# First mixer of a two-layer trunk: silu in one instruction for eight convolution tiles, the softplus chain behind them, q's products of both token tiles ahead of rotary and turns

## The chip, the cores and the metric

The kernel runs on one core of a Trainium2 chip. The metric is the device time of one execution in microseconds. The kernel before takes 1034.35 us, the median of three runs (1034.08 to 1034.95).

## The reference

A decoder trunk of two layers works on 256 tokens of width 1024, in float32. Each layer is half a SwiGLU block, a mixer, and another half block, all added to the residual. The change lies in the first mixer alone:

```
z, xbc, dt, q_a, kv_a = split(h @ w_in)
xbc = silu(causal_conv4(xbc) + conv_b)          # 2048 channels: xs 1024, B 512, C 512
dt  = softplus(dt + dt_bias)                    # 16 heads
y   = ssd(xs, dt, -exp(a_log), B, C) + d_skip * xs
y   = rms_norm_by_group(y * silu(z))
q   = rope(rms_norm(rms_norm(q_a) @ w_q_b))     # 8 heads of 96, the last 32 rotary
k,v = rms_norm(kv_c) @ w_kv_b ...               # 8 heads of 64 + 32 shared rotary, 8 of 64
o   = causal_softmax_attention(q, k, v)
out = concat(y, o) @ w_out
```

In ssd, the decay between two tokens of a chunk of 128 is exp(acs[i] − acs[j]), where acs is the running sum of dt·A within the chunk.

## The kernel before

Activations lie as 128 tokens by channels (two token tiles, t = 0 and 1) or turned as 128 channels by 256 tokens. A float32 product is made of three products of two-part operands (high and low part, names ending in h and l, or wh and wl for weights); ScalarE casts the high part of each weight tile (L77) and VectorE makes the low part (L80).

In the first mixer the work goes in this order. The products into q_a and kv_a (two token tiles). Then convolution tiles: `xbc(c)` makes one of 16 channel tiles, 24 matmuls of 256 columns into a bank p_xbc; `conv_silu` (L441) reads it: ScalarE writes cv (Identity with scale and bias, L446), VectorE adds three taps (L448), ScalarE takes Tanh (L451), VectorE makes (tanh + 1)·v (L452). The convolution's weights are halved beforehand, so v is half of the convolution and (tanh v + 1)·v is silu of the whole. Tiles 8 to 11 are B (tile BT), 12 to 15 are C (tile CT), 0 to 7 are xs (tile xT).

Between them stand the products of q by heads (bank p_qb, two per token tile, L279 to L281, each read by Square L532, the copy qnat L534 and the copy qr L535), the rotary step on POOL, the turns m_qT, the products of k and v (p_kvb) and their turns m_kT.

The softplus chain: Abs (L395) and Exp (L398) on ScalarE, a polynomial of nine VectorE steps (L402), dts, a (L587), the matmul m_acs (L590) that sums a over the chunk, the turn m_acsT, ScalarE's copy acsT (L597), and a transfer on POOL's queue to acs_rows in DRAM (L599). From there two transfers per token tile (L657, POOL's queue) spread the rows of 8 heads each to all partitions as E. On E ScalarE does 16 Relus of one head each (L663) and four Exps (L666), VectorE multiplies by the products CB (L669), and TensorE uses it in m_yd (L703).

Attention goes by token tile: scores m_sc into PSUM banks of 512 columns (two buffers; 4 heads a bank for t = 0, 2 heads for t = 1), the maximum on VectorE, Exp on ScalarE (p, L629), 1/den on VectorE and the product by it on POOL (L424), turns m_pT, then m_att_o.

Later the z products (p_z, four tiles of 512 columns), their gates (ScalarE Tanh L715, VectorE L716), the gated norm, and the product out of the mixer (p_acc, L323 to L325), which reuses the banks of z.

All instructions of one engine run in order. The order is not the program's: a scheduler that simulates a timeline puts each engine's instructions in a row and hands out buffers, and `self.order(a, b)` adds that a comes after b. So an edit at one place can move instructions at another.

Of the kernel before, what the change touches and what calls it, by code (L numbers as in the profile page):

```python
# [11 lines left out]
AF = mybir.ActivationFunctionType  # L12
# [3 lines left out]
P = 128  # L16
# [18 lines left out]
ROW = {}  # L35
# [50 lines left out]
class Net:  # L86
# [351 lines left out]
        return pt  # L438


    def conv_silu(self, c, b, out):  # L441

        nc = self.nc
        cw = self.conv[:, c, :]
        v = self.small([P, S], "cv", bufs=3)
        nc.scalar.activation(out=v, in_=b, func=AF.Identity, scale=cw[:, 3:4], bias=cw[:, 4:5])  # L446
        for s in (1, 2, 3):
            nc.vector.scalar_tensor_tensor(out=v[:, s:], in0=b[:, :S - s], scalar=cw[:, 3 - s:4 - s], in1=v[:, s:],  # L448
                                           op0=ALU.mult, op1=ALU.add)
        th = self.small([P, S], "cth", bufs=2)  # L450
        self.tanh = nc.scalar.activation(out=th, in_=v, func=AF.Tanh)  # L451
        return nc.vector.scalar_tensor_tensor(out=out, in0=th, scalar=1.0, in1=v, op0=ALU.add, op1=ALU.mult)  # L452
# [12 lines left out]
    def mixer0(self, hT, x, after):  # L465
        nc, st, row = self.nc, self.st, self.row
# [5 lines left out]
        dtv = self.small([P, 2, 16], "dtv")  # L472
# [5 lines left out]
        for t in range(2):  # L478
            c = slice(t * P, (t + 1) * P)
# [8 lines left out]
            squares = nc.scalar.activation(out=junk[:, :32], in_=pk[:, 256:], func=AF.Square, accum_out=ssn[:, t, 2:3])  # L488
            nc.vector.tensor_scalar(out=ssn[:, t, 0:2], in0=ssn[:, t, 0:2], scalar1=EPS, scalar2=None, op0=ALU.add)
            self.power(rsn[:, t, :], ssn[:, t, 0:2])  # L490
            qn = self.blk([P, 640], "qn", grp="a")
# [12 lines left out]
        BC = [self.blk([P, 4, S], n) for n in ("BT", "CT")]  # L504

        def xbc(c, out):
            w = st.load([D])[0]
            b = self.bank([P, S], "xbc")
            self.in_ch(b, hT, w)
            return self.conv_silu(c, b, out)  # L510
        for i in range(4):
            xbc(8 + i, BC[0][:, i, :])

# [4 lines left out]
        qT = [self.blk([96, 8, P], f"qT{t}", grp="a") for t in range(2)]  # L518
        kT = [self.blk([96, 8, P], f"kT{t}", grp="a") for t in range(2)]
        sq = self.small([P, 2, 8], "sqs")  # L520
        for t in range(2):
            qn = self.blk([P, 8, 96], "qnat", grp="a")
            qr = self.blk([P, 8, 2, 16], "qr")
            for j in range(2):
                b = self.bank([P, 4, 96], "qb")
                bf = b.rearrange("p a b -> p (a b)")
                for k in range(3):
                    self.mm_tok(bf, lambda k: (qaT[0][:, k, :], qaT[1][:, k, :]), [k], t,
                                [(wq[k][0][:, j * 384:(j + 1) * 384], wq[k][1][:, j * 384:(j + 1) * 384])], k == 0, k == 2)
                hs = slice(4 * j, 4 * j + 4)  # L530
                junk = self.small([P, 512], "junk")[:, :384].rearrange("p (a b) -> p a b", a=4)
                nc.scalar.activation(out=junk, in_=b, func=AF.Square)  # L532
                nc.vector.tensor_reduce(out=sq[:, t, hs], in_=junk, op=ALU.add, axis=X)
                nc.scalar.copy(out=qn[:, hs, :64], in_=b[:, :, :64])  # L534
                nc.scalar.copy(out=qr[:, hs, :, :], in_=b[:, :, 64:].rearrange("p a (s d) -> p a s d", s=2))  # L535
            roped = self.apply_rope(qn[:, :, 64:].rearrange("p a (s d) -> p a s d", s=2), qr, t, "q", 8)

            nc.vector.tensor_scalar(out=sq[:, t, :], in0=sq[:, t, :], scalar1=96 * EPS, scalar2=None, op0=ALU.add)
            self.power(sq[:, t, :], sq[:, t, :])
            self.order(self.pow, roped)  # L540
            for j in range(2):
                tp = self.tbank([96, 4, P], "qT", "a")
                for i in range(4):
                    self.transpose(tp[:, i, :], qn[:, 4 * j + i, :])
                nc.scalar.copy(out=qT[t][:, 4 * j:4 * j + 4, :], in_=tp)
        xbc(12, BC[1][:, 0, :])
        wkv = st.load([D, D])
        for t in range(2):
# [6 lines left out]
            for j in range(2):  # L555
                b = self.bank([P, 4, P], "kvb")
# [16 lines left out]
            for j in range(2):  # L573
# [2 lines left out]
                    self.transpose(tp[:, i, :], kn[:, 4 * j + i, :])  # L576
                nc.scalar.activation(out=kT[t][:, 4 * j:4 * j + 4, :], in_=tp, func=AF.Copy, scale=self.kgain)


        e = self.small([P, 2, 16], "dte")  # L580
        l1 = self.log1p_exp(dtv, e, "dtl", squares)
        dts = self.edge.tile([P, 2, 16], F32, tag="dts", name="dts", bufs=1)
        nc.vector.scalar_tensor_tensor(out=dts, in0=dtv, scalar=0.0, in1=l1, op0=ALU.max, op1=ALU.add)
        ea = self.small([P, 16], "ea")
        nc.scalar.activation(out=ea, in_=row[:, ROW["a_log"]], func=AF.Exp)
        a = self.small([P, 32], "a")
        nc.vector.scalar_tensor_tensor(out=a.rearrange("p (t h) -> p t h", t=2), in0=dts, scalar=-1.0,  # L587
                                       in1=ea.unsqueeze(1).broadcast_to([P, 2, 16]), op0=ALU.mult, op1=ALU.mult)
# [10 lines left out]
        nc.gpsimd.dma_start(out=rows, in_=at_)  # L599
        eacs = self.small([P, 16], "eacs")  # L600
        nc.scalar.activation(out=eacs, in_=acs[:, 16:], func=AF.Exp)

        for i in (2, 3):
            xbc(12 + i, BC[1][:, i, :])


        den = self.small([P, 2, 8], "den")
# [3 lines left out]
        def softmax(t):  # L611
            n = 4 >> t
            kw = P * (t + 1)
            pr = [self.blk([P, 8 // (t + 1), kw], f"p{t}", grp="a") for _ in range(t + 1)]
            for j in range(8 // n):
                b = self.sbank([P, n, kw], "sc", "a")
                for i in range(n):
                    h = n * j + i
                    for kb in range(t + 1):
                        mm(b[:, i, kb * P:(kb + 1) * P], qT[t][:, h, :], kT[kb][:, h, :], start=i == 0 and kb == 0, stop=False,  # L620
                           skip_group_check=True)
                mm(b, self.identb, self.mask[:, 2 * P - kw:].unsqueeze(1).broadcast_to([P, n, kw]), start=False, stop=True, skip_group_check=True)
                hs = slice(n * j, n * j + n)
                nc.vector.tensor_reduce(out=mx[:, t, hs], in_=b, op=ALU.max, axis=X)
                nc.vector.scalar_tensor_tensor(out=mx[:, t, hs], in0=mx[:, t, hs], scalar=-1.0, in1=sq[:, t, hs], op0=ALU.mult, op1=ALU.mult)
                for i in range(n):
                    h = n * j + i
                    m = 8 // (t + 1)
                    self.exp = nc.scalar.activation(out=pr[h // m][:, h % m, :], in_=b[:, i, :], func=AF.Exp, scale=sq[:, t, h:h + 1],  # L629
                                                    bias=mx[:, t, h:h + 1], accum_out=den[:, t, h:h + 1])  # L630
                m = 8 // (t + 1)
                h = n * j
                self.normalize(pr[h // m][:, h % m:h % m + n, :], den[:, t, hs])
            for kb in range(t + 1):
                PT[t, kb] = self.turn_probs(lambda h: pr[h // m][:, h % m, kb * P:(kb + 1) * P], kb, f"pT{t}{kb}")
        oT = [self.blk([P, 2, 4, P], f"oT{t}", F32R, grp="a") for t in range(2)]
        exps = []
        for t in range(2):
            softmax(t)
            exps.append(self.exp)  # L640
            self.attend(t, lambda b, h: PT[t, b][:, h, :], lambda b, h: V[:, b, h, :],
                        (oT[t][:, 0], oT[t][:, 1]))
# [66 lines left out]
        for j in range(2):  # L709
            wz = [s for _ in range(2) for s in st.load([D, D])]  # L710
            for t in range(2):
                b = self.bank([P, 512], "z")
# [39 lines left out]
        for j, (s, hs) in enumerate(cols):  # L752
            nc.gpsimd.tensor_tensor(out=hv(xd[0][:, s]), in0=hv(xd[0][:, s]), in1=dec[:, hs].unsqueeze(2).broadcast_to([P, 8, 64]), op=ALU.mult)
            b = self.sbank([P, 512], "st", "b")
# [3 lines left out]
        for j, (s, hs) in enumerate(cols):  # L758
            b = self.sbank([P, 512], "yo", "b")
# [414 lines left out]
```

## Time and profile before

| | us |
|---|---|
| median of three runs | 1034.35 |
| the profiled execution | 1034.39 |
| its span, first to last instruction | 1032.6 |
| TensorE busy | 1011.2 |
| VectorE busy | 686.0 |
| ScalarE busy | 568.6 |
| POOL busy | 83.8 |

The profile is of one execution. Busy time counts an engine's instructions; what is left of TensorE's span, 21.4 us, is idle time, and the view of waits says on which line it stood and which instruction released it. A timeline lists an engine's instructions by start; a bracket behind a row gives the idle time before it and its releaser. The granted TensorE clock was 0.997 of 2.4 GHz on average.

### The profile page before, as it was taken

The numbers are of one execution on the slowest core, as the hardware profiler recorded it, in microseconds if no ns is written. First come the engines' busy times: TensorE is split into PE (matmuls) and PEld (weight loads), VectorE is DVE, ScalarE is ACT, GpSimd is POOL, SyncE is SP. The second block draws the span as 40 slices with busy tenths as digits, with TensorE's granted clock in tenths as the row PEclk, the third lists the DMA queues.
The fourth block names the chain that finished last, engine by engine and source line by source line (L and its number), as shares of the span: only waits on it lengthen the run. The fifth ranks groups of instructions, "written<-read, shape, count | busy, mean of one in ns | idle before, by whom it ended". The sixth has DMA issues, their size and how long they took to land.

```text
span 1032.6 us, 15136 instructions
## 1 busy us (share of the span) xinstructions
PE 1011.2 (98%) x5609; PEld 866.7 (84%) x5609; DVE 686.0 (66%) x1056; ACT 568.6 (55%) x1036; POOL 83.8 (8%) x110
## 2 busy tenths in 40 slices
PE   6999999999999999999999999999999899999998
PEld 5888888898988888888888888888887678888886
DVE  6877754598786767677437776753688567666641
ACT  5665553487866465655425656543556346555530
POOL 2100000017131200000000000000113200000000
PEclk9999999999999999999999999999999899999999
DMA  8776655464454367555554756655372356555451
GB/s 299 261 219 194 188 185 186 128 213 173 152 171 155 101 206 244 194 193 186 190 176 147 258 187 189 196 189 164 123 235 94 101 163 195 193 183 185 154 192 41
DMA packets 52090, 185.95 MB, mean 180 GB/s; under 512 B 5911, under 2 KB 5928, under 8 KB 52016
## 3 DMA queue, kind: packets, MB, share of 16 engines
q1 hardware_dynamic: 49248, 176.58, 52.3%
q0 software_dynamic: 2048, 6.83, 2.0%
q10 hardware_dynamic: 720, 1.57, 0.4%
q8 instruction: 44, 0.72, 0.3%
q14 instruction: 30, 0.25, 0.1%
HBM read 183.89 MB, written 1.06 MB: 179 GB/s over the span
## 4 chain that ended last, share of the span: by engine, by line
PE 93%; ACT 2%; DMA 2%; DVE 2%; issue 1%; POOL 1%; DVEq 0%; POOLq 0%; ACTq 0%
PE p_u L307 13%; PE p_g L307 13%; PE p_acc L324 10%; PE p_acc L323 10%; PE p_acc L325 10%; PE p_u L308 7%; PE p_g L308 7%; PE p_u L281 1%; PE p_u L280 1%; PE p_u L279 1%; PE p_g L279 1%; PE p_g L280 1%; PE p_g L281 1%; PE m_nrm L119 1%; DVE wl L80 1%
## 5 line engine op out<-in xcount | busy, mean ns | idle before, releaser
L80 DVE TENSOR_TENSOR wl<-raw,wh 128x1024 fp32r<-128x1024 f32 (+3 forms) x341 | 413.8, 1225 | 222.8 <-ACT wh L77 221.2
L77 ACT CAST wh<-raw 128x1024 fp32r<-128x1024 f32 (+3 forms) x341 | 351.5, 1039 | 297.6 <-PE p_acc L324 102.3
L307 PE MATMUL p_u<-hT,wh 128*128 128x512 f32 x576 | 204.1, 393 | 0.0
L307 PE MATMUL p_g<-hT,wh 128*128 128x512 f32 x576 | 204.0, 393 | 0.0
L308 PE MATMUL p_u<-hT,wl 128*128 128x256 f32 x576 | 161.7, 281 | 0.0
L308 PE MATMUL p_g<-hT,wl 128*128 128x256 f32 x576 | 161.5, 280 | 0.0
L325 PE MATMUL p_acc<-wl,acth 128*128 128x512 f32 x352 | 137.1, 389 | 0.0
L324 PE MATMUL p_acc<-wh,actl 128*128 128x512 f32 x352 | 137.0, 389 | 0.0
L323 PE MATMUL p_acc<-wh,acth 128*128 128x512 f32 x352 | 136.2, 391 | 0.0
L307 PEld LDWEIGHTS p_g<-hT,wh 128*128 128x128 f32 x576 | 107.9, 187 | 24.5
L307 PEld LDWEIGHTS p_u<-hT,wh 128*128 128x128 f32 x576 | 107.9, 187 | 24.4
L308 PEld LDWEIGHTS p_g<-hT,wl 128*128 128x128 f32 x576 | 108.8, 189 | 0.2
L308 PEld LDWEIGHTS p_u<-hT,wl 128*128 128x128 f32 x576 | 108.8, 189 | 0.0
L325 PEld LDWEIGHTS p_acc<-wl,acth 128*128 128x128 f32 x352 | 66.1, 188 | 13.8
L323 PEld LDWEIGHTS p_acc<-wh,acth 128*128 128x128 f32 x352 | 66.1, 188 | 13.6
L324 PEld LDWEIGHTS p_acc<-wh,actl 128*128 128x128 f32 x352 | 66.1, 188 | 13.4
L236 POOL TENSOR_TENSOR ss<-ss,mhalf 128x1 f32<-128x1 f32 x12 | 6.7, 559 | 576.7 <-DVE ss L254 576.7
L331 DVE SCALAR_TENSOR_TENSOR x<-p_acc,x 128x512 f32<-128x512 f32 x24 | 16.4, 688 | 38.0 <-PE p_acc L325 38.0
L296 PE MATMUL p_xbc<-hT,wh 128*128 128x256 f32 x128 | 36.9, 288 | 0.8 <-DVE cv L448 0.8
L298 PE MATMUL p_xbc<-hT,wl 128*128 128x256 f32 x128 | 36.6, 286 | 0.0
L297 PE MATMUL p_xbc<-hT,wh 128*128 128x256 f32 x128 | 36.2, 283 | 0.0
L383 DVE TENSOR_TENSOR sg<-sg 128x256 f32<-128x256 f32 x72 | 30.6, 425 | 7.9 <-DVE sg L380 0.9
(370 smaller groups left out, 1513.7 us busy)
## 6 DMA issues: line engine op xcount, KB each, us to landing
raw<-in_w SPq DMA_DIRECT2D x326, 512.0 KB, 4.2
gain<-in_gains POOLq DMA_DIRECT2D x5, 512.0 KB, 5.2
E<-acs_rows POOLq DMA_DIRECT2D x4, 512.0 KB, 6.2
raw<-in_w SPq DMA_DIRECT2D x4, 400.0 KB, 3.2
raw<-in_w SPq DMA_DIRECT2D x4, 288.0 KB, 2.9
raw<-in_w SPq DMA_DIRECT2D x3, 384.0 KB, 3.6
raw<-in_w SPq DMA_DIRECT2D x4, 272.0 KB, 2.8
out<-x ACTq DMA_DIRECT2D x4, 256.0 KB, 2.0
```

The costliest lines, as they stand in the source:

```text
L77: self.cast = nc.scalar.copy(out=hi, in_=raw)
L80: nc.vector.tensor_tensor(out=lo, in0=raw, in1=hi.bitcast(F32), op=ALU.subtract)
L279: mm(out, ah, wh, start=first and i == 0, stop=False)
L296: mm(out, hi[:, cs], xh, start=k == 0, stop=False)
L297: mm(out, hi[:, cs], xl, start=False, stop=False)
L298: mm(out, lo[:, cs], xh, start=False, stop=k == KT - 1)
L307: mm(out, hi[:, cs], hT[k // 2][:, k % 2], start=k == 0, stop=k == KT - 1, skip_group_check=True)
L308: mm(out[:, 0, :], lo[:, cs], self.hk(hT, k)[0], start=False, stop=k == KT - 1, skip_group_check=True)
L323: first = nc.tensor.matmul(o, ah, w[0][:, s], start=k == 0, stop=False)
L324: nc.tensor.matmul(o, al, w[0][:, s], start=False, stop=False)
L325: nc.tensor.matmul(o, ah, w[1][:, s], start=False, stop=k == nk - 1)
L383: nc.vector.tensor_tensor(out=sg, in0=sg, in1=v[:, 1, :], op=ALU.mult)
```

## The change

Three edits, all in `mixer0` and `conv_silu`. For tiles c ≥ 8 (B and C) `conv_silu` takes one ScalarE Silu of 2·v in place of Tanh and the VectorE product. The products of q by heads and the copies out of their banks are written for both token tiles before the rotary step, the normalisation and the turns, with two buffers for qnat and qr each. The softplus chain stands behind the last two C tiles, its Abs and its Exp of a_log are ordered behind the last Silu, and so is the first Exp of the attention.

```diff
--- before.py
+++ after.py
@@ -438,7 +438,8 @@
         return pt
 
 
-    def conv_silu(self, c, b, out):
+    def conv_silu(self, c, b, out, table):
+
 
         nc = self.nc
         cw = self.conv[:, c, :]
@@ -447,6 +448,9 @@
         for s in (1, 2, 3):
             nc.vector.scalar_tensor_tensor(out=v[:, s:], in0=b[:, :S - s], scalar=cw[:, 3 - s:4 - s], in1=v[:, s:],
                                            op0=ALU.mult, op1=ALU.add)
+        if table:
+            self.silu = nc.scalar.activation(out=out, in_=v, func=AF.Silu, scale=2.0)
+            return self.silu
         th = self.small([P, S], "cth", bufs=2)
         self.tanh = nc.scalar.activation(out=th, in_=v, func=AF.Tanh)
         return nc.vector.scalar_tensor_tensor(out=out, in0=th, scalar=1.0, in1=v, op0=ALU.add, op1=ALU.mult)
@@ -507,7 +511,7 @@
             w = st.load([D])[0]
             b = self.bank([P, S], "xbc")
             self.in_ch(b, hT, w)
-            return self.conv_silu(c, b, out)
+            return self.conv_silu(c, b, out, c >= 8)
         for i in range(4):
             xbc(8 + i, BC[0][:, i, :])
 
@@ -518,9 +522,11 @@
         qT = [self.blk([96, 8, P], f"qT{t}", grp="a") for t in range(2)]
         kT = [self.blk([96, 8, P], f"kT{t}", grp="a") for t in range(2)]
         sq = self.small([P, 2, 8], "sqs")
-        for t in range(2):
-            qn = self.blk([P, 8, 96], "qnat", grp="a")
-            qr = self.blk([P, 8, 2, 16], "qr")
+        qns = [self.blk([P, 8, 96], "qnat", grp="a") for _ in range(2)]
+        qrs = [self.blk([P, 8, 2, 16], "qr") for _ in range(2)]
+        for t in range(2):
+            qn = qns[t]
+            qr = qrs[t]
             for j in range(2):
                 b = self.bank([P, 4, 96], "qb")
                 bf = b.rearrange("p a b -> p (a b)")
@@ -533,6 +539,8 @@
                 nc.vector.tensor_reduce(out=sq[:, t, hs], in_=junk, op=ALU.add, axis=X)
                 nc.scalar.copy(out=qn[:, hs, :64], in_=b[:, :, :64])
                 nc.scalar.copy(out=qr[:, hs, :, :], in_=b[:, :, 64:].rearrange("p a (s d) -> p a s d", s=2))
+        for t in range(2):
+            qn, qr = qns[t], qrs[t]
             roped = self.apply_rope(qn[:, :, 64:].rearrange("p a (s d) -> p a s d", s=2), qr, t, "q", 8)
 
             nc.vector.tensor_scalar(out=sq[:, t, :], in0=sq[:, t, :], scalar1=96 * EPS, scalar2=None, op0=ALU.add)
@@ -576,13 +584,16 @@
                     self.transpose(tp[:, i, :], kn[:, 4 * j + i, :])
                 nc.scalar.activation(out=kT[t][:, 4 * j:4 * j + 4, :], in_=tp, func=AF.Copy, scale=self.kgain)
 
+        for i in (2, 3):
+            xbc(12 + i, BC[1][:, i, :])
+
 
         e = self.small([P, 2, 16], "dte")
-        l1 = self.log1p_exp(dtv, e, "dtl", squares)
+        l1 = self.log1p_exp(dtv, e, "dtl", self.silu)
         dts = self.edge.tile([P, 2, 16], F32, tag="dts", name="dts", bufs=1)
         nc.vector.scalar_tensor_tensor(out=dts, in0=dtv, scalar=0.0, in1=l1, op0=ALU.max, op1=ALU.add)
         ea = self.small([P, 16], "ea")
-        nc.scalar.activation(out=ea, in_=row[:, ROW["a_log"]], func=AF.Exp)
+        self.order(nc.scalar.activation(out=ea, in_=row[:, ROW["a_log"]], func=AF.Exp), self.silu)
         a = self.small([P, 32], "a")
         nc.vector.scalar_tensor_tensor(out=a.rearrange("p (t h) -> p t h", t=2), in0=dts, scalar=-1.0,
                                        in1=ea.unsqueeze(1).broadcast_to([P, 2, 16]), op0=ALU.mult, op1=ALU.mult)
@@ -599,9 +610,6 @@
         nc.gpsimd.dma_start(out=rows, in_=at_)
         eacs = self.small([P, 16], "eacs")
         nc.scalar.activation(out=eacs, in_=acs[:, 16:], func=AF.Exp)
-
-        for i in (2, 3):
-            xbc(12 + i, BC[1][:, i, :])
 
 
         den = self.small([P, 2, 8], "den")
@@ -628,6 +636,8 @@
                     m = 8 // (t + 1)
                     self.exp = nc.scalar.activation(out=pr[h // m][:, h % m, :], in_=b[:, i, :], func=AF.Exp, scale=sq[:, t, h:h + 1],
                                                     bias=mx[:, t, h:h + 1], accum_out=den[:, t, h:h + 1])
+                    if t == h == 0:
+                        self.order(self.exp, self.silu)
                 m = 8 // (t + 1)
                 h = n * j
                 self.normalize(pr[h // m][:, h % m:h % m + n, :], den[:, t, hs])
```

On ScalarE, around the first Exps of the second token tile's attention. In before, E_266 and E_267 are the two halves of E for t = 0, and their Relus (L663) stand ahead of the Exps (L629) of t = 0 (p_237):

```order
L446 ACTIVATE cv_2879<-p_xbc_2854,conv_140 128x256
L451 ACTIVATE cth_2603<-cv_2598 128x256
L577 ACTIVATE kT_172_2237<-m_kT_2521,kgain_151 96x512
L577 ACTIVATE kT_172_2237<-m_kT_2527,kgain_151 96x512
L663 ACTIVATE E_266_2811<-E_266_2811,acs_2555 128x128 x7
L451 ACTIVATE cth_2642<-cv_2637 128x256
L663 ACTIVATE E_267_2812<-E_267_2812,acs_2555 128x128 x8
L446 ACTIVATE cv_2918<-p_xbc_2893,conv_140 128x256
L77 CAST wh_1_3256<-raw_1_3254 128x1024
L451 ACTIVATE cth_2884<-cv_2879 128x256
L666 ACTIVATE E_266_2811<-E_266_2811 128x512
L666 ACTIVATE E_267_2812<-E_267_2812 128x512
```

Now, with E_258 and E_259 for the same halves, p_238 for the first half of t = 1, and m_sc_2690, 2703 and 2716 its first three banks of scores:

```order
L608 COPY acsT_2621<-m_acsT_2619 32x128
L231 CAST oT_227_2631<-m_att_o_2677 128x512
L455 ACTIVATE cth_2946<-cv_2941 128x256
L447 ACTIVATE cv_2980<-p_xbc_2955,conv_140 128x256
L447 ACTIVATE cv_3036<-p_xbc_3011,conv_140 128x256
L447 ACTIVATE cv_3075<-p_xbc_3050,conv_140 128x256
L77 CAST wh_0_3326<-raw_0_3324 128x1024
L673 ACTIVATE E_258_2795<-E_258_2795,acs_2617 128x128 x7
L637 ACTIVATE p_238_2688,den_2629<-m_sc_2690,mx_2630,sqs_2230 128x256 x2
L673 ACTIVATE E_258_2795<-E_258_2795,acs_2617 128x128
L673 ACTIVATE E_259_2796<-E_259_2796,acs_2617 128x128 x4
L676 ACTIVATE E_258_2795<-E_258_2795 128x512
```

The Relus on E moved from ahead of the Exps of t = 0 to directly ahead of the first Exps of t = 1, a few places behind the copy of acsT.

On POOL, around the transfer to acs_rows. In before it stands between the k work of the two token tiles, ahead of the normalisation of t = 0 (p_237):

```order
L571 TENSOR_TENSOR knat_2394<-pr_2395,rk_2402 128x8x32
L461 TENSOR_TENSOR pr_2484<-pe_1907,cgk_204 128x16 x2
L463 TENSOR_TENSOR pr_2484<-pr_2484,rtmp_210_2485 128x32
L790 MEMSET gaT_7131 17x256
L599 DMA acs_rows<-acsT_2559 32x128
L236 TENSOR_TENSOR rk_2491<-rk_2491,mhalf_81 128x8
L571 TENSOR_TENSOR knat_2483<-pr_2484,rk_2491 128x8x32
L657 DMA E_266_2811<-acs_rows 128x1024
L657 DMA E_267_2812<-acs_rows 128x1024
```

Now it stands behind both normalisations (p_229) of t = 0:

```order
L236 TENSOR_TENSOR rk_2479<-rk_2479,mhalf_81 128x8
L579 TENSOR_TENSOR knat_2471<-pr_2472,rk_2479 128x8x32
L424 TENSOR_TENSOR p_229_2633<-p_229_2633,rden_231_2646 128x512
L424 TENSOR_TENSOR p_229_2633<-p_229_2633,rden_233_2661 128x512
L800 MEMSET gaT_7115 17x256
L610 DMA acs_rows<-acsT_2621 32x128
L667 DMA E_258_2795<-acs_rows 128x1024
L667 DMA E_259_2796<-acs_rows 128x1024
L424 TENSOR_TENSOR p_238_2688<-p_238_2688,rden_241_2700 128x512
```

The transfers of E follow the one to acs_rows directly, and all three moved behind the attention of t = 0.

On ScalarE, ahead of the gates. In before the gates' Tanhs (L715) of three z tiles stand behind the second half of E for t = 1 (E_307):

```order
L437 COPY pT_259_2771<-m_pT_2778 128x512
L663 ACTIVATE E_307_3221<-E_307_3221,acs_2555 128x128 x8
L666 ACTIVATE E_307_3221<-E_307_3221 128x512
L715 ACTIVATE gate_3297<-p_z_3272 128x512
L715 ACTIVATE gate_3325<-p_z_3300 128x512
L715 ACTIVATE gate_3377<-p_z_3352 128x512
```

Now, with E_298 and E_299 the two halves for t = 1:

```order
L673 ACTIVATE E_298_3204<-E_298_3204,acs_2617 128x128 x8
L77 CAST wh_1_3598<-raw_1_3596 128x1024
L77 CAST wh_0_3616<-raw_0_3614 128x1024
L676 ACTIVATE E_298_3204<-E_298_3204 128x512
L77 CAST wh_1_3622<-raw_1_3620 128x1024
L676 ACTIVATE E_298_3204<-E_298_3204 128x512
L673 ACTIVATE E_299_3205<-E_299_3205,acs_2617 128x128 x8
L725 ACTIVATE gate_3281<-p_z_3256 128x512
L725 ACTIVATE gate_3309<-p_z_3284 128x512
L725 ACTIVATE gate_3361<-p_z_3336 128x512
```

The first half of E for t = 1 and three casts now stand close ahead of the gates as well.

## Rows read from the trace of the kernel before

**Rows 1.** The page, part 1: busy time and share of each engine

```profile
PE 1011.2 (98%) x5609; PEld 866.7 (84%) x5609; DVE 686.0 (66%) x1056; ACT 568.6 (55%) x1036; POOL 83.8 (8%) x110
```

**Rows 2.** TensorE's waits, whole span: line, releaser, us, times, longest

```profile
PE m_pT L119 <- POOL p L424: 1.3, 1, 1.3
PE p_qb L279 <- ACT qr L535: 1.0, 1, 1.0
...
PE p_xbc L296 <- DVE cv L448: 0.8, 1, 0.8
PE p_kvb L279 <- ACT qr L535: 0.7, 1, 0.7
...
PE m_acs L590 <- DVE a L587: 0.5, 1, 0.5
```

**Rows 3.** ScalarE's timeline: start us, us, line, operation, out<-in [idle before <-releaser]

```profile
251.62 0.24 ACT L597 COPY acsT<-m_acsT 32x128 f32<-32x128 f32 x1
...
262.69 2.16 ACT L663 ACTIVATE E<-E,acs 128x128 f32<-128x128 f32 x7 [0.46 <-DMA E<-acs_rows]
...
291.33 0.56 ACT L629 ACTIVATE p<-m_sc,mx,sqs 128x256 f32<-128x256 f32 x1 [1.40 <-DVE mx L625]
...
291.88 0.55 ACT L629 ACTIVATE p<-m_sc,mx,sqs 128x256 f32<-128x256 f32 x1
...
307.91 2.44 ACT L663 ACTIVATE E<-E,acs 128x128 f32<-128x128 f32 x8 [2.06 <-DMA E<-acs_rows]
310.26 1.13 ACT L666 ACTIVATE E<-E 128x512 f32<-128x512 f32 x2
...
314.69 2.45 ACT L663 ACTIVATE E<-E,acs 128x128 f32<-128x128 f32 x8 [0.74 <-DMA E<-acs_rows]
...
317.56 1.53 ACT L715 ACTIVATE gate<-p_z 128x512 f32<-128x512 f32 x3
...
319.98 2.96 ACT L77 CAST wh<-raw 128x1024 fp32r<-128x1024 f32 x3
```

**Rows 4.** POOL's timeline, the same columns

```profile
252.15 0.61 POOL L599 DMA_DIRECT2D acs_rows<-acsT  x1 [3.77 <-ACT acsT L597]
...
255.09 1.30 POOL L571 TENSOR_TENSOR knat<-pr,rk 128x256 f32<-128x256 f32 x1
256.47 1.14 POOL L657 DMA_DIRECT2D E<-acs_rows  x2
...
301.78 0.60 POOL L657 DMA_DIRECT2D E<-acs_rows  x1 [0.24 <-PE p_z L280]
...
310.66 0.59 POOL L657 DMA_DIRECT2D E<-acs_rows  x1 [2.65 <-PE m_yd L703]
```

**Rows 5.** The view of transfers: queue, count, KB, us to landing

```profile
acs_rows<-acsT POOLq DMA_DIRECT2D x1, 16.0 KB, 4.0
```

**Rows 6.** The view of tile E, its last line

```profile
DMA to landing us min/median/max: 3.9/6.2/6.8
```

**Rows 7.** TensorE's timeline around the first scores

```profile
263.89 0.28 PE L298 MATMUL p_xbc<-hT,wl 128*128 128x256 f32 x1
264.01 1.06 PE L620 MATMUL m_sc<-kT,qT 96*128 96x128 f32 x8
...
265.12 1.05 PE L620 MATMUL m_sc<-kT,qT 96*128 96x128 f32 x8
```

**Rows 8.** TensorE's timeline in the second mixer

```profile
809.61 0.63 PE L323 MATMUL p_acc<-wh,oT 128*128 128x512 f32 x1
810.04 0.63 PE L324 MATMUL p_acc<-wh,oT 128*128 128x512 f32 x1
...
810.99 0.39 PE L324 MATMUL p_acc<-wh,oT 128*128 128x512 f32 x1
811.22 0.39 PE L325 MATMUL p_acc<-wl,oT 128*128 128x512 f32 x1
```

**Rows 9.** Windows, second mixer: busy time by engine, PEclk, DMA share, GB/s

```profile
805.70:810.50 4.80, 4.79 (x14) 3.92 (x15) 2.93 (x6) 0.00 (x0) 0.00 (x0) 0.50 0.82 272
```

## The prediction

> **What bounds the kernel now.** I read the page first: TensorE is busy 1011.2 of 1032.6 us, VectorE 686.0, ScalarE 568.6 [rows 1]. The reader is to see that only TensorE's standing still counts; an instruction taken from VectorE or ScalarE is worth nothing unless TensorE waited for it. The view of TensorE's waits comes next [rows 2]. Four of its lines lie in the changed stretch (the first mixer, some 205 to 362 us): 1.0 us in the products of q by heads and 0.7 in those of k and v, both until ScalarE has copied qr out of a PSUM bank; 0.8 in a convolution tile; 0.5 at the matmul m_acs. Together 3.0 us: no reordering here can win more than that and some tenths for restarts.
>
> Then I read the path on which the softplus result goes, through ScalarE, POOL and the DMA queues [rows 3 to 6]. The turned sums acsT are copied at 251.62 (0.24 us); POOL issues the transfer to acs_rows at 252.15, which lands 4.0 us later, and behind its k work issues the two transfers that spread these rows into E, at 256.47. ScalarE's first Relu on E starts at 262.69, having waited 0.46 us for the transfer: 6.2 us from issue to landing, which is also the median of the four [rows 6]. So the chain of two dependent transfers had almost no reserve before, even with acsT ready at 251.9.
>
> **The change part by part.**
>
> *Eight Tanh and eight VectorE products become eight Silu.* The products leave VectorE, which is off the path. On ScalarE one instruction replaces one. Order shows one table load as before, now behind the last Silu. I cost it at nothing; what hides it is TensorE's queue of tiles.
>
> *The copies of all four q banks stand together.* In before ScalarE copied the banks of the second token tile only behind the first turns, and the k and v product waited 0.7 us for that [rows 2]. Now they follow their own matmuls: this wait goes. The first q wait stays: it is the second product of the first token tile that wants the bank of the one before it, which the edit doesn't touch.
>
> *The softplus chain moves behind the last Silu.* m_acs leaves its place among the products of k and v, and its 0.5 us wait goes [rows 2]. But everything that hangs on it moves too. The turn of acs is now behind the fifth of the tiles that hold x, and the copy of acsT follows it; I put that at about 277.0, with the turn ending at 276.5, by adding up, from the second scores on, the pitches of what stands in TensorE's queue (0.12 us for a 256-column matmul, 1.1 for a bank of scores) [rows 7]. That is 25 us later than 251.62.
>
> What is queued behind it decides. In before the eight Exps of the first token tile stood behind the E Relus, and those of the second tile from 291.33 on [rows 3]. In the new order seven Relus on E stand directly ahead of the first Exps of the second token tile. ScalarE runs in order, so these Exps wait for E. The third bank of scores of that tile reuses the PSUM bank which these Exps read, and TensorE, in order too, stands at it, with an x tile and the z products behind.
>
> The size of this wait, from the end of the turn: ScalarE's copy and POOL's issue 0.8 (251.62 to 252.15 is 0.53, with the hand-over before it), acs_rows 4.0, POOL's next issue 0.2 (it has nothing else in between), E 6.2, seven Relus 2.2 (2.16), two Exps 1.1 (291.33 to 291.88 is 0.55), hand-over 0.1: 14.6 us [rows 3, 4]. TensorE meanwhile has 16 matmuls of 0.12 (1.9), two banks of scores (2.2) and some 18 small ones, an estimate of 2.4 from their places elsewhere: 6.5, so it asks for the bank at 283.0. **Stall 8.1 us.** With the fastest E transfer, 3.9 [rows 6], it is 5.8; with the slowest, 6.8, it is 8.7.
>
> A rule speaks for less. The Trainium skill, "DMA: Bandwidth & Descriptors", section "Anatomy of one DMA — SWDGE (gpsimd) path", gives a transfer on POOL's queue a fixed 2.0 us plus its bytes over 436 GB/s; by that an estimate of 2.0 for acs_rows and 3.2 for E, and a stall of 3.1. The trace doesn't agree: 4.0 for the 16 KB, and 3.9 at the least for E [rows 5, 6]. The sum goes by the trace.
>
> While TensorE stands at the third scores, what made it wait before is done: the products' 0.7, m_acs's 0.5 and the convolution tile's 0.8 lie ahead of or inside this stall and no longer add. With their restarts I credit 2.5. Net of the first place: 8.1 − 2.5 = +5.6.
>
> *The clock.* In the second mixer TensorE stood 1.3 us for a normalised p among other short waits [rows 2], and from 803.8 on the granted clock was 0.50, the 1.2 GHz level; 512-column matmuls then came every 0.43 us (809.61 to 810.04) in place of 0.23 (810.99 to 811.22) [rows 8]. It rose again after 4.8 us of dense work [rows 9], 11 such matmuls at 0.20 more: 2.2 us. A stall of 6 us or more is longer than any that dropped the clock there, so I add **+2.2**; from below it is 0, if the clock stays.
>
> *The second place.* The first products of the way out (p_acc) reuse the bank of the first z tile, which VectorE's gate product reads last, behind ScalarE's gate Tanh. In before those Tanhs came at 317.56, with a whole z tile (24 matmuls) still ahead of p_acc on TensorE. Now they stand behind E of the second token tile, both halves. The first half's transfer is issued when TensorE is three matmuls into the last z tile (before: 301.78, behind POOL's normalisation). From there: issue and landing 0.3 + 6.1 (301.78 to 307.91), eight Relus 2.4, three casts about 2.9 (2.96 at 319.98), two Exps 1.1, eight Relus 2.4, Tanh 0.5 (1.53 for three), VectorE's product 0.7: 16.4 us [rows 3, 4]. TensorE has 11.8 by the pitches: the rest of that z tile (21 at 0.23), the attention product, the state products, CB and the turn of B. Stall 4.6; with a landing of 4.0 (310.66 to 314.69) 2.5, and then ScalarE's copies of xs and VectorE's cb bound it at about 2.4. Between the ends I take 3.4, and take off 0.4 for before's own short waits behind this place: **+3.0**.
>
> What comes behind (the gated norm, the turns of y, the second pass through POOL's power) has shorter queues in the new order than before and I give it 0, from −1 to +2.
>
> **The sum.** 5.6 + 2.2 + 3.0 = +10.8 us. Against the profiled execution (1034.39, its span 1032.6 and 1.8 around it, and 0.04 above the median of 1034.35) that is 1045.2.
>
> **The rivals.**
>
> *The gains alone.* E lands before TensorE needs the third scores, and only the waits for qr and a go. For it: ScalarE waited for E only 0.46 us before, so transfers and orders were in step there. Against: E cannot land before acsT plus 4.0 plus 3.9, which is 285.4, while TensorE wants the bank at 283.0 and the Relus and Exps take 3.3 before. It decides at an acsT copied by about 269 instead of 277. Price: −0.7 − 0.5 and restarts of 0.3, so −1.5, or −2.5 with the convolution tile's wait: 1032.3. Faster.
>
> *Balance.* A quick E (3.9), no drop of the clock, and most of the second place hidden since the whole rest moved back with it: 5.8 − 2.5 is already +3.3, so the second scores must come some 2 us later than I put them, or the turn of acs earlier: 1033 to 1036. By the rule of the Trainium skill's page "DMA: Bandwidth & Descriptors" above, the first place would be +0.6, near this case.
>
> *One stall, full clock.* The first place as forecast, 8.1 − 2.5, and the clock stays up since transposes and weight loads keep some activity at its edges; the second place falls to its lower end, of which POOL's and ScalarE's later work absorbs half. +5.6 + 1.2: 1041.
>
> *A third wait.* The slow E (8.7), a clock that falls at both places (2 × 2.2), the second at 4.6, and the gated norm 2 late: 6.2 + 4.4 + 4.2 + 2 = +16.8: 1051.
>
> **How the numbers follow.** Chances: forecast 0.50, one stall with full clock 0.22, gains alone 0.12, balance 0.07, third wait 0.09. Without the gains case the likeliest one's own range is 1039 to 1049. The range from 1034.5 to 1050.0 leaves out the gains alone (0.12), a part of the balance (0.02) and a part of the third wait (0.04). A measurement of this kernel can tell 0.2% (2.1 us) from no change. Faster by that: nearly all of the gains case and none of the others, 0.12. Within it: the balance's larger part and a little of the rest, 0.08. Slower: 0.80.
>
> **What would show it.** Right: in TensorE's waits the line of the scores (L628) appears, held by ScalarE's p (L637), with 5 to 9 us in one piece near 283; ScalarE's Relu on E (L673) stands some 3 to 6 us idle until the E transfer; the transfer to acs_rows is issued at about 277 instead of 252; the lines of the kvb products and of m_acs are gone, the qb line stays near 1.0; the granted clock is 0.50 for 4 to 7 us just behind; p_acc (L323) waits 2 to 5 us for the gate (L726). Wrong: the Relus on E start without idle time, or the scores' banks come free in time; then the gains case holds. If the stall is there and the time still falls, my credit for what TensorE no longer waits for was too small.

## The result, and the profile after

The changed kernel takes 1044.87 us (median of four runs, 1044.11 to 1045.89) against 1034.21 of the kernel before on the same chip: a ratio of 1.0105, 95% interval 1.0093 to 1.0117, so some 10.7 us slower. The profiled execution took 1045.22, its span 1043.4.

The page after, its first and its clock line, answer to [rows 1]:

```profile
PE 1014.6 (97%) x5609; PEld 869.2 (83%) x5609; DVE 685.1 (66%) x1048; ACT 570.0 (55%) x1036; POOL 85.5 (8%) x110
...
PEclk9999999999988999999999999999999899999999
```

TensorE is busy 3.4 us more and stands idle 28.8 us in place of 21.4. The clock line falls below 9 in the two slices from 287 to 339 us, in the first mixer (and in the second mixer, as before).

TensorE's waits in the first mixer (200 to 385 us; line, releaser, us, times, longest), which answer to [rows 2]:

```profile
PE m_sc L628 <- ACT p L637: 4.5, 1, 4.5
PE p_acc L323 <- DVE gate L726: 3.3, 1, 3.3
PE p_qb L279 <- ACT qr L541: 1.5, 1, 1.5
PE m_Bn L119 <- DVE xs L714: 0.6, 1, 0.6
```

The waits of p_kvb, m_acs and p_xbc are gone and p_qb's grew from 1.0 to 1.5. (Before has a fifth wait in this mixer, 0.4 us of p_acc for yT, which is gone too.) Three lines are new; two of them make up 7.8 us, the scores for p and the way out for the gate.

ScalarE's timeline at the two places, for [rows 3]:

```profile
276.84 0.26 ACT L608 COPY acsT<-m_acsT 32x128 f32<-32x128 f32 x1 [0.57 <-PE m_acsT L119]
...
285.25 2.15 ACT L673 ACTIVATE E<-E,acs 128x128 f32<-128x128 f32 x7 [2.03 <-DMA E<-acs_rows]
287.31 0.55 ACT L637 ACTIVATE p<-m_sc,mx,sqs 128x256 f32<-128x256 f32 x1
...
320.45 2.45 ACT L673 ACTIVATE E<-E,acs 128x128 f32<-128x128 f32 x8
...
326.69 2.43 ACT L673 ACTIVATE E<-E,acs 128x128 f32<-128x128 f32 x8
329.02 1.54 ACT L725 ACTIVATE gate<-p_z 128x512 f32<-128x512 f32 x3
```

acsT is copied at 276.84. ScalarE's next E row starts at 285.25, after 2.03 us idle for the transfer, and only behind its seven Relus come the Exps on which the scores' bank hangs. Forty us later the gates' Tanhs at 329.02 stand behind both halves of the next E. VectorE's product of the gate, which p_acc waits for, comes only at 330.91, behind cb and two products on E:

```profile
330.91 1.88 DVE L726 SCALAR_TENSOR_TENSOR gate<-gate,p_z 128x512 f32<-128x512 f32 x3
```

POOL's timeline, for [rows 4], and E's landings, for [rows 6]:

```profile
277.38 0.61 POOL L610 DMA_DIRECT2D acs_rows<-acsT  x1 [4.01 <-ACT acsT L608]
280.80 1.09 POOL L667 DMA_DIRECT2D E<-acs_rows  x2 [2.81 <-DMA acs_rows<-acsT]
...
316.60 0.60 POOL L667 DMA_DIRECT2D E<-acs_rows  x1 [8.22 <-PE p_z L281]
...
319.53 0.53 POOL L667 DMA_DIRECT2D E<-acs_rows  x1 [1.82 <-PE m_xsT L119]
```

```profile
DMA to landing us min/median/max: 3.8/4.8/6.0
```

TensorE's timeline at both places:

```profile
283.65 0.38 PE L119 MATMUL m_xsT<-sq,xT 128*128 128x128 f32 x2
288.55 2.07 PE L628 MATMUL m_sc<-kT,qT 96*128 96x128 f32 x8 [4.52 <-ACT p L637]
...
327.74 0.65 PE L119 MATMUL m_Bn<-sq,BT 128*128 128x128 f32 x4 [0.60 <-DVE xs L714]
331.64 0.79 PE L323 MATMUL p_acc<-wh,oT 128*128 128x512 f32 x1 [3.25 <-DVE gate L726]
332.23 0.63 PE L324 MATMUL p_acc<-wh,oT 128*128 128x512 f32 x1
332.66 0.63 PE L325 MATMUL p_acc<-wl,oT 128*128 128x512 f32 x1
```

It stood 4.52, 0.60 and 3.25 us. Behind the second stall 512-column products come every 0.43 us, as in [rows 8].

Windows around both (busy us of PE, PEld, DVE, ACT, POOL, each with its count; then granted clock, DMA share, GB/s), for [rows 9]:

```profile
285.90:292.60 6.70, 4.05 (x18) 3.90 (x19) 3.21 (x9) 6.70 (x23) 1.59 (x3) 0.50 0.25 82
292.70:300.00 7.30, 7.30 (x41) 6.35 (x40) 5.03 (x8) 5.02 (x14) 2.40 (x4) 1.00 0.01 1
330.30:337.00 6.70, 5.36 (x13) 4.20 (x14) 6.39 (x13) 4.16 (x13) 0.72 (x1) 0.50 0.22 75
337.10:344.00 6.90, 6.90 (x37) 5.83 (x36) 1.55 (x5) 1.40 (x3) 1.27 (x2) 1.00 0.24 76
```

Each stall is followed by a stretch at 0.50, the 1.2 GHz level, in which TensorE did 4.05 and 5.36 us of work.

From the last product into p_u ahead of the mixer to the first behind it TensorE takes 229.8 us in before and 240.2 in after, 10.4 more. A ledger of these, an estimate made by taking from each start-to-start distance on TensorE the usual one for its size: the scores' stall +4.7; the turn of B +0.8; the gate's stall +3.4; the first half clock +2.0, the second +2.6; p_qb +0.5; gone are p_kvb's 0.8, m_acs's 0.7, the convolution tile's 1.0 and the 0.6 at yT, and 0.4 of smaller restarts.

### The profile page after: what moved, and what is told of

Read it like the earlier page. It is cut to its first block, busy times and chain, and to the rows that moved or that the text cites. A ratio compares the mean times of both kernels' runs of the same rounds, so it can differ in the third digit from the quotient of the medians.

```text
span 1043.4 us, 15135 instructions
## 1 busy us (share of the span) xinstructions
PE 1014.6 (97%) x5609; PEld 869.2 (83%) x5609; DVE 685.1 (66%) x1048; ACT 570.0 (55%) x1036; POOL 85.5 (8%) x110
## 4 chain that ended last, share of the span: by engine, by line
PE 91%; DVE 3%; DMA 2%; ACT 2%; issue 2%; POOL 0%; DVEq 0%; ACTq 0%; POOLq 0%
PE p_u L307 13%; PE p_g L307 13%; PE p_acc L324 10%; PE p_acc L323 10%; PE p_acc L325 10%; PE p_u L308 7%; PE p_g L308 7%; DVE wl L80 2%; PE p_u L281 1%; PE p_u L280 1%; PE p_u L279 1%; PE p_g L279 1%; PE p_g L280 1%; PE p_g L281 1%; DMA raw<-in_w 1%
```

## The experiments

My theory: the loss is two places where ScalarE, in order, holds work that TensorE needs behind work on E. Rivals: a late softplus chain costs by itself; Silu or its table; the q edit; or the waits only change their names if one is removed.

### Parts of the change alone

**q_alone**: before, with this edit of the change alone.

```diff
-        for t in range(2):
-            qn = self.blk([P, 8, 96], "qnat", grp="a")
-            qr = self.blk([P, 8, 2, 16], "qr")
+        qns = [self.blk([P, 8, 96], "qnat", grp="a") for _ in range(2)]
+        qrs = [self.blk([P, 8, 2, 16], "qr") for _ in range(2)]
+        for t in range(2):
+            qn, qr = qns[t], qrs[t]
...
+        for t in range(2):
+            qn, qr = qns[t], qrs[t]
             roped = self.apply_rope(
```

> Before, with q's copies of both token tiles alone moved ahead of rotary and turns; Tanh and the early softplus chain stay. My theory: only the 0.7 us wait of the k and v product for qr goes, with its restart 0.8, so about 1033.4; m_acs's 0.5 and the convolution tile's 0.8 stay. A rival: the scheduler moves other work with it and new waits eat the gain, 1034 to 1036.

1040.84 us, ratio 1.0061 (1.0044 to 1.0078). My theory of the edit missed by 7 us. TensorE's waits and ScalarE's row on E:

```profile
PE m_sc L624 <- ACT kT L581: 2.8, 1, 2.8
PE m_sc L624 <- DVE oT L232: 1.6, 1, 1.6
PE p_qb L279 <- ACT qr L537: 1.0, 1, 1.0
```

```profile
267.30 2.15 ACT L667 ACTIVATE E<-E,acs 128x128 f32<-128x128 f32 x7 [6.11 <-DMA E<-acs_rows]
269.36 1.03 ACT L77 CAST wh<-raw 128x1024 fp32r<-128x1024 f32 x1
270.30 0.68 ACT L581 ACTIVATE kT<-m_kT,kgain 96x512 f32<-96x512 f32 x1
```

The wait of p_kvb for qr did go. But the scheduler now put seven Relus ahead of the copies kT, and ScalarE stood 6.11 us in front of them, with nothing else allowed past; the scores waited 2.8 us for kT. The granted clock was 0.50 for 3.4 us behind each of the two score waits. So the same trap seems to exist with the early chain, by the Relus' place and not by how late acsT is; q_fix below tests it.

**silu_alone**: before with Silu for c ≥ 8, chain and q's copies where they were.

```diff
-            return self.conv_silu(c, b, out)
+            return self.conv_silu(c, b, out, c >= 8)
```

> Before with eight Silu in place of Tanh and product, softplus chain and q's copies where they were. Now the chain's Exps fall between Silus, and ScalarE loads its table four times in the mixer instead of once. My theory: three loads more, 1.28 us each, fall into ScalarE's idle times, no wait on TensorE above 1.5 us is new: 1033 to 1036. The rival (a load delays the copies that free banks, or the scheduler's new order puts E ahead of what TensorE wants, as with the q edit alone): 1038 to 1042.

1043.11 us, ratio 1.0087 (1.0071 to 1.0104): the rival. Five table loads stand in this mixer in place of one (I had counted four), 1.28 us each. New waits on TensorE: 2.8 us of a convolution tile, 1.6 more at p_qb, twice 1.0 at CB and kT, 0.6 in the products of k and v; the clock was 0.50 for 3.4 us behind the first two. The trace shows a load (227.57) and the first Silu ahead of the copies out of p_qb, whose qr comes at 230.40 in place of 229.01, and seven Relus that stand 3.59 us idle for E ahead of the Silu which CB waits for. So both parts of the rival are in it; no run tells what each cost.

**tanh_q**: the changed kernel with Tanh for all tiles.

```diff
-            return self.conv_silu(c, b, out, c >= 8)
+            return self.conv_silu(c, b, out, False)
```

(and `self.silu` read as `self.tanh` in the three orders)

> The changed kernel with Tanh and VectorE's product kept for all 16 tiles; the late softplus chain (behind the last of these Tanhs) and the q edit stay. The scheduler puts the first two Exps of the second token tile ahead of the Relus on E here. My theory: the loss is the late chain's and not Silu's, so this is also slower than before, by the second place at least (p_acc for the gate 3 to 5 us and a half clock of 2): 1038 to 1044. The rival (Silu makes the loss): within 1.5 us of before.

1045.39 us, ratio 1.0107 (1.0092 to 1.0122), above my range by 1.4. As slow without Silu: the loss doesn't need the eight Silu. Waits: p_acc for the gate 4.7, the scores for p still 1.8, though the two Exps do stand ahead of the Relus here; they come behind a weight cast, a Tanh and two reads of convolution banks. The clock was 0.50 for 6.8 us at the first and 3.4 at the second place.

**silu_chain**: the changed kernel without the q edit.

```diff
+        for t in range(2):
+            qn = self.blk([P, 8, 96], "qnat", grp="a")
+            qr = self.blk([P, 8, 2, 16], "qr")
```

> The changed kernel without the q edit: eight Silu, the softplus chain behind them, copies of q as before. The chain is as late as in the changed kernel, but the scheduler puts the first two Exps of the second token tile ahead of all Relus on E. My theory (the stall needs the Relus ahead of the Exps that free the scores' bank): no wait of the third scores, the clock stays full there, the wait for qr (0.7) comes back, the wait of p_acc for the gate (3 to 4 us, with a half clock behind it) stays: about 1039, range 1036 to 1042. The rival (a chain 25 us later costs by itself, wherever the Relus stand): 1044 to 1047.

1044.22 us, ratio 1.0097 (1.0082 to 1.0112): by its time the rival, by its trace half of each. The third scores don't wait, as I had said, and no half clock stands there; but the second pair of Exps is now behind all 16 Relus (293.04), and the turns of p wait 2.9 us for the last pair (304.29), which comes behind VectorE's maximum and two casts. At the second place 4.1 and 1.8 us, with 6.8 us at 0.50.

```profile
PE p_acc L323 <- DVE gate L722: 4.1, 1, 4.1
PE m_pT L119 <- ACT p L633: 2.9, 1, 2.9
PE m_Bn L119 <- DVE xs L710: 1.8, 1, 1.8
```

### Taking away each wait

**e_all**: all Relus on E of the first token tile behind the last Exp of the second. The program orders only the first of the 16, the others are free to run ahead.

```diff
-                    if g == i == 0:
-                        self.order(first, exps[t])
+                    if t == 0 or g == i == 0:
+                        self.order(first, exps[1])
```

> The changed kernel with all 16 Relus on E of the first token tile ordered behind the last Exp of the second token tile. My theory: the wait of the scores for p (4.5 us) and the half clock behind it (some 2 us) go, the second place (p_acc for the gate) stays or grows by up to 2: 1036 to 1040. The rival (TensorE would wait at that place for something else, as the transfer or the Exps are only the last to come): no gain over 1 us, 1043 to 1046.

1044.53 us, ratio 1.0098 (1.0081 to 1.0114): the scores' wait fell from 4.5 to 0.4 and the clock there stayed full, as expected, but nothing came out at the end. The time is the rival's, not by its reason: the second place grew by 3.8 us, where I had allowed 2. TensorE's waits:

```profile
PE p_acc L323 <- DVE gate L726: 7.1, 1, 7.1
...
PE m_CB L661 <- DVE xs L714: 0.9, 1, 0.9
PE m_sc L628 <- ACT p L637: 0.4, 1, 0.4
```

```profile
317.09 2.45 ACT L673 ACTIVATE E<-E,acs 128x128 f32<-128x128 f32 x8 [3.40 <-DMA E<-acs_rows]
...
327.17 1.54 ACT L725 ACTIVATE gate<-p_z 128x512 f32<-128x512 f32 x3
```

```profile
328.18 2.49 DVE L679 TENSOR_TENSOR E<-E,cb 128x512 f32<-128x512 f32 x4
330.59 1.87 DVE L726 SCALAR_TENSOR_TENSOR gate<-gate,p_z 128x512 f32<-128x512 f32 x3
```

TensorE came to p_acc 4.2 us earlier (its last turn of B began at 324.0 in place of 328.1) and waited 7.1 there. The gates' Tanhs are set by ScalarE's own queue behind the second E: 327.17, only 1.9 us earlier than in the changed kernel. And of these 1.9 only 0.3 reached TensorE, since VectorE, in order too, now had a weight's low part and all four products on E ahead of the gate's product: 330.59 in place of 330.91. So at the second place work on E stands ahead of the gate on two engines.

**gates_first**: the changed kernel with z and gates written ahead of E of the second token tile.

```diff
-        E1 = decays(1)
         gate = {}
...
+        E1 = decays(1)
         sn = self.blk([P, D], "ssmn", grp="a")
```

> The changed kernel with the z products and gates written ahead of E of the second token tile, so that the gates' Tanhs stand ahead of its Relus on ScalarE. My theory: the first stall (4.5 us) and the half clock behind it stay as they are, the 3.3 us wait of p_acc for the gate, its half clock (2.5) and most of the 0.6 at the turn of B go: 1038 to 1040. The rival (the wait moves on: E of the second token tile is late for its own products, or the norm for the turns of y): 1042 to 1046.

1041.5 us, ratio 1.0076 (1.0059 to 1.0092), between my range and the rival's. The gate's wait, the turn of B's and the second half clock are gone; the scores wait 5.2 in place of 4.5. Of the 6.8 us of the second place 3.4 were won in time: 0.7 went to the longer stall, and the profiled execution takes 0.7 more between the two mixers. Where the rest went is open.

**e_all_gates**: both of these edits.

> The changed kernel with both edits: the 16 Relus on E of the first token tile behind the last Exp of the second, and the z products and gates written ahead of E of the second token tile. With the first alone the third scores' wait went from 4.5 to 0.4 us but p_acc's wait for the gate grew from 3.3 to 7.1; with the second alone the gate's wait went and the scores' stayed at 5.2. My theory (two queues on ScalarE, each with its own stall, the later one taking over what the earlier gives back): without either only the first q wait and the wait for yT are left, 1033 to 1036. The rival (ScalarE's work between acsT and the gated norm is itself too long, so a third wait appears, at the state products or the turns of y): 1038 to 1042.

1034.13 us, ratio 0.9996 (0.9987 to 1.0005): back at before, with all three parts of the change in it. The chain is as late as in the changed kernel (acsT copied at 276.48), so neither its lateness nor the Silu cost anything that these runs could tell. The two queues on E, the first on ScalarE, the second on ScalarE and VectorE, are the whole loss, and they hide each other: alone they give 0.3 and 3.4 us, together 10.7. What is left:

```profile
PE p_qb L279 <- ACT qr L541: 1.5, 1, 1.5
PE p_xbc L296 <- DVE cv L449: 0.9, 1, 0.9
PE p_acc L323 <- ACT yT L231: 0.5, 1, 0.5
PE m_sc L628 <- ACT p L637: 0.4, 1, 0.4
PE m_CB L661 <- DVE xs L714: 0.3, 1, 0.3
```

**e_mid_gates**: as e_all_gates, the Relus behind the fourth Exp of the second token tile.

```diff
+                    if t == 1 and h == 3:
+                        self.mid = self.exp
...
-                        self.order(first, exps[1])
+                        self.order(first, self.mid if t == 0 else exps[1])
```

> As the run with both edits, but the Relus stand behind the fourth Exp of the second token tile, so that E is ready some 5 us earlier. My theory: both stalls gone, 1033 to 1036, and against the other run no difference above 1 us, since E is then early enough in both. The rival (E of the first token tile is late for its products): this one 1.5 to 4 us faster than the other.

1041.58 us, ratio 1.0071 (1.0056 to 1.0086): neither of my two cases. Both old stalls are gone, but the Tanh that xT needs and the attention's oT fell behind Relus on E of the second token tile on ScalarE, and the copy Bn behind work of the gated norm. TensorE waits 2.1 us for Bn, 1.5 for oT and 1.0 for xT, with two half clocks. So an order that mends both places can still lose 7 us at others.

### The same orders without the change

**q_fix**: q_alone with the Relus behind the first token tile's own Exps.

```diff
-                    if g == i == 0:
+                    if t == 0 or g == i == 0:
                         self.order(first, exps[t])
```

> The q edit alone (Tanh and early chain kept), and all 16 Relus on E of the first token tile ordered behind its last Exp; the program so far ordered only the first of them. With the q edit alone seven Relus stood 6.1 us idle on ScalarE for the transfer, ahead of the copies kT that the scores wait for (2.8 us on TensorE, two half clocks). My theory: that wait and its clock go, so 1034 to 1037, unless a wait at the gates appears, since the Tanhs now stand behind E of the second token tile. The rival (the q edit loses by its copies' place, not by E): 1039 to 1042.

1033.7 us, ratio 0.9991 (0.9981 to 1.0001): 7.1 us won by moving the Relus alone, and neither score wait is left. This shows the cause of q_alone's loss.

**before_fix_gates**: before, with that line and gates_first's move, none of the change.

> Before, none of the three edits of the change, with the two orders alone: Relus on E of the first token tile behind its Exps, z products and gates ahead of E of the second. My theory: the convolution tile's wait (0.8), which came at the end of a chain through those Relus, goes, the others stay: 1033 to 1035. The rival (before's order was good by chance and any edit of E loses): 1037 to 1041.

1035.73 us, ratio 1.001 (1.0001 to 1.002), a little slower. The convolution tile's wait went, as expected (before's five waits in this mixer are now four), and the median is above my range by 0.7. Of the 1.6 us that its profiled execution takes more than before's, 0.4 lie in the first mixer and the others behind it.

**q_fix_gates**: q_fix with gates_first's move.

> The same with the z products and gates written ahead of E of the second token tile. My theory: no wait on E or on a gate is left, and those for qr of the k and v product and of the convolution tile are gone, m_acs's 0.5 and the first q wait stay: 1032 to 1034, so 0 to 2 us faster than before. The rival (a further wait appears in the scheduler's new order, as in five of eight kernels so far): 1036 to 1041.

1030.77 us, ratio 0.9965 (0.9952 to 0.9977): faster than both kernels, and below my range by 1.2. TensorE waits in the mixer for 1.7 us in all:

```profile
PE p_qb L279 <- ACT qr L537: 1.0, 1, 1.0
PE p_z L279 <- DVE gate L719: 0.5, 1, 0.5
PE p_xbc L296 <- DVE cv L448: 0.2, 1, 0.2
```

```profile
268.45 0.46 ACT L633 ACTIVATE p<-m_sc,mx,sqs 128x128 f32<-128x128 f32 x1 [2.15 <-DVE mx L629]
...
273.34 4.81 ACT L667 ACTIVATE E<-E,acs 128x128 f32<-128x128 f32 x16
```

The Exps start first, and the 16 Relus run in one piece with no idle time for the transfer. Between the same two products into p_u the mixer takes 227.2 us against 229.8 in before: 2.6 of the 3.5 us by which the profiled spans differ. The other 0.9 lie outside the changed stretch, 0.5 of them in the second mixer, where the granted clock was at 0.50 for 3.4 us in place of 6.8; as it was also in silu_chain and others, with other edits, they aren't credited to this one.

## Why the prediction was right

The two places, their causes and their releasers were as forecast. The time (1045.2 forecast, 1044.9 measured) was nearly exact by luck: two terms were off by some 3.5 us each, one too large and one too small.

- *The waits that go.* p_kvb's, m_acs's and the convolution tile's are gone, 2.5 us by the ledger, which was the credit; 0.6 at yT went as well, for the 0.4 taken off the second place. The first q wait stayed but grew by 0.5, which wasn't forecast.
- *The late acsT.* Forecast 277.0, measured 276.84; the transfer's issue 277.38. The place, the cause and the releaser of the scores' wait (L628 by p L637) were as forecast, and e_all shows that the Relus ahead of these Exps make it.
- *The size of the first stall was mis-sized*: 8.1 forecast, 4.5 idle and 4.7 with the restart measured, below even the lower end of 5.8. ScalarE's idle time for the transfer was 2.03, below the 3 to 6 that I had named as a sign. The two transfers were quicker: from issue 277.38 POOL could issue E at 280.80 (3.4 with hand-overs, for 4.0 and 0.2) and ScalarE started at 285.25 (4.45 for 6.2). And TensorE asked for the bank at 284.03, 1.0 later than the 283.0 of the sum. I took 6.2, since it was the same transfer; but its time varies from kernel to kernel. The windows from issue to first Relu, in before, after and q_alone (the last two numbers are the DMA engines' busy share and GB/s):

```profile
256.50:262.70 6.20, 6.20 (x55) 6.20 (x55) 5.49 (x11) 3.93 (x8) 1.10 (x2) 1.00 0.79 275
```

```profile
280.80:285.20 4.40, 3.23 (x27) 2.87 (x25) 4.40 (x11) 2.39 (x4) 1.09 (x2) 1.00 0.69 247
```

```profile
258.60:267.30 8.70, 8.70 (x76) 8.70 (x75) 5.18 (x11) 1.82 (x3) 1.76 (x3) 1.00 0.84 276
```

  Between E's first issue and the first Relu two weight loads were issued in before, two in q_alone and none in after; the same transfer took 6.2, 8.65 and 4.45. So the loads may explain the quick one, but not what parts the other two; no run isolates it. The rule of the Trainium skill, "DMA: Bandwidth & Descriptors", section "Anatomy of one DMA — SWDGE (gpsimd) path", gave an estimate of 3.2 for E: the fastest of these rows, 4.45, lies between it and mine. The stall of 3.1 that the prediction set against its own by this rule was nearer to the measured 4.5 than my 8.1.
- *The clock.* 2.2 forecast for the first place and 2.0 measured. But it fell at the second place as well, at a stall of 3.25 us, and cost 2.6 there, which I had only in the rival of a third wait.
- *The second place.* 3.4 forecast, 3.25 idle (3.4 with the restart) for the same releaser, the gate. That agreement is luck in part: the first Relus started 3.85 us after the transfer's issue (316.60 to 320.45), where the longer sum had 6.4, and the gate's product stood behind cb and two products on E on VectorE, which that sum left out. The 0.6 at the turn of B just ahead, behind VectorE's sum of xs, wasn't forecast. With this and the clock the place cost 6.8 in place of 3.4.

Sum as measured: first place 4.7 − 2.6 = 2.1, its clock 2.0, the second place 6.8, smaller restarts −0.4: 10.5.

The rivals: the gains alone would have needed Relus that don't stand ahead of the Exps, as in e_all_gates, and even there the time was only before's. "One stall, full clock" and "balance" both assumed a clock that stays; it fell at both.

## What to carry to other kernels

Where an engine runs in order and a scheduler sets its row, look at what stands behind each instruction that waits for a transfer: TensorE was stopped not by the transfer but by an Exp or a copy queued behind a Relu that waited for it. Then look at the next engine on the way too: in e_all VectorE's products on E held the gate when ScalarE no longer did. An order given for the first of 16 alike instructions leaves the other 15 free; give it to all that wait. And take away two such places together before giving up on either: here each alone gave 0.3 to 3.4 us and both 10.7, and parts of a change that look harmless (the q edit) lost 6.6 us through the new order and, with both places reordered, ended 3.9 below before, of which 2.6 show in the changed stretch.

## What the runs showed of the hardware

Transfers of the same 512 KB on POOL's queue took from 3.6 to 10.2 us within one execution (tile E in q_alone, least and most of four), so a single landing is a poor price:

```profile
DMA to landing us min/median/max: 3.6/8.1/10.2
```

The granted clock fell to 0.50, the 1.2 GHz level, at stalls of 4.5 and 3.25 us in after, in q_alone at 2.8 and 1.6 us, and in e_mid_gates behind 1.0 and 1.5 us close together. It stayed full in before, where no wait of this mixer was above 1.0, in q_fix behind one of 1.5, and in silu_chain at one of 2.9 (the 3.0 us from 302.6 hold 0.13 us of TensorE's work):

```profile
302.60:305.60 3.00, 0.13 (x2) 0.06 (x2) 3.00 (x7) 2.53 (x7) 0.54 (x1) 1.00 0.66 201
305.60:312.00 6.40, 6.40 (x33) 5.37 (x34) 5.53 (x11) 1.26 (x3) 1.04 (x1) 1.00 0.71 238
```

So the length of one stall doesn't tell whether the clock falls. How long it stays low varies too: 6.8 us in the second mixer of before and 3.4 in that of q_fix_gates, behind the same two waits of p and oT.
